# First layer's last MLP quarter by seven products, and the next layer's adaLN columns in the output projection, in a two-layer diffusion trunk

## The chip, the cores and the metric

One Trainium2 chip, one core. The time is device microseconds of one execution. TensorE (PE) multiplies, VectorE (DVE) and ScalarE (ACT) work on the operands and results, GpSimd (POOL) and SyncE (SP) issue transfers from HBM.

## What is computed

Two layers on 640 tokens (128 context and 512 latent) of width 1024, in fp32. Each layer is, cut to what matters here:

```
mod = silu(cond) @ w_ada[l] + b_ada[l]              # adaLN: sh1, sc1, g1, sh2, sc2, g2, 1024 each
h   = rms_norm(x, norm1_g) * (1 + sc1) + sh1
m   = mixers(h @ w_in)                               # FNet, GQA, differential attention, gated chunk MLP
x   = x + g1 * (sum(sigmoid(h @ w_gate) * branches) @ w_out)
h   = rms_norm(x, norm2_g) * (1 + sc2) + sh2
f   = square(relu(h @ w_mlp1)) @ w_mlp2              # 1024 -> 4096 -> 1024
x   = x + g2 * f
```

A final RMSNorm follows the second layer.

## The kernel before

**Tiles.** x is kept transposed in eight tiles `xT[m]` of 128 features by 640 tokens; HN = 320 is half the tokens. Every weight and operand is split into a rounded part and the rest, and each product of a block is three matmuls (`mm3`, line 807): high by high, low by high, high by low. So for every weight block of 128 x 1024 ACT makes a rounded copy (`whi`) and VectorE subtracts it to get `wlo`; `Stream.pump` (line 332) does this ahead. Weights come by SP into `raw` buffers. Those that a seven-product block needs as a sum of two blocks come into `chain` buffers, the second load adding to the first, issued on GpSimd's queue.

**The order of the work** is set by a planner at build time. Each engine has an estimated clock. The main program issues TensorE's matmuls. Generators in numbered lanes (norms, sums, attention, adaLN) are stepped from `tick` (line 617) whenever TensorE's clock has passed the time at which they are due; `tick` first lets the weight stream pump, then steps the lanes. What is issued later on an engine stands behind what was issued before.

**A layer.** First projection of h (`bq_bkv`, line 1010: query and key/value columns of branch B, token tile by token tile), other projections and attention, gates and branches, output projection (`units_of` for feature tiles 0 and 1, then `tail`, line 831, for tiles 2 to 7 in two halves of the tokens), norm, MLP.

**The MLP** has four quarters q of 1024 hidden columns. Each has a block m1 (by w_mlp1) and a block m2 (by w_mlp2). A block is a 2 x 2 matrix product by seven products p1 to p7 instead of eight (the Strassen-Winograd scheme; `block`, line 2064). A product is 48 matmuls of 320 columns: two pairs of output tiles, four inner tiles, three matmuls. Its operands p5, p6, p3, p7, p4 are sums of the operand's quarters, made and split by `sums` (line 1926) in a lane; p1 and p2 are quarters themselves (`hh`, `hl` of h; `fh`, `fl` of f). The order of the products is p1, p2, p5, p6, p7, p3, p4. `m1_read` squares the relu and makes the quarters of f; `m2_read` (line 2154) adds g2 times the result to xT.

**The exception** is m2 of q = 3. It is done plainly: the first four feature tiles by `units_of` (192 matmuls of 320 columns), the last four by `tail` with the token parts (0, 256) and (256, 640): 96 matmuls of 256 and 96 of 384 columns. m1 of q = 3 therefore makes `fhi` and `flo` for all of f instead of operands of seven products. In layer 0 the next layer's adaLN set 0 (its first 2048 columns: `ada_run`, line 701, eight steps of four matmuls, each with two loads of 512 KB issued two steps ahead, then four transposes and an addition) is spawned there and interleaves with the first 192 matmuls. The norm for the next layer (`norm_part`, line 764) starts for the first 256 tokens once their part is done. It is: sums of squares by TensorE (`ones,sq`), a reciprocal square root in twelve tiny VectorE operations on `small`, a broadcast by TensorE (`ident,small`), then for each of eight k `ht` (VectorE), `hhi` (ACT), `hlo` (VectorE). Layer 1's first projection takes token tiles 0, 1 and then 2, 3, 4.

**The norm before the MLP** (`mlp_rstd`, line 1978, and `mlp_h`) has the same steps for each half; the second half's are done during p1 of the first m1 block. All units of 128 x 1280 come from one pool of 30.

## Time and profile before

| | us |
|---|---|
| median of three runs (2069.89 to 2070.89) | 2069.9 |
| the profiled execution | 2070.2 |
| its span | 2068.4 |
| TensorE busy | 2009.4 (97%) |
| VectorE busy | 1322.5 (64%) |
| ACT busy | 1009.0 (49%) |
| GpSimd busy | 212.9 (10%) |

The span is the time between the first and the last instruction in the trace; the execution's own time is 1.8 us longer. A row of the table of stretches gives a stretch's limits, its length, each engine's busy time with the number of instructions, the granted TensorE clock (1.00 is the upper level, 2.4 GHz; a part of a stretch at 1.2 GHz lowers the mean), the DMA engines' busy share and what they moved. In layer 0 the output projection ends at 612.13 us, the first m1 block's p1, p2, p5, p6, p7 follow up to 659.12. The last m1 block's p4 begins at 961.84, plain m2 at 969.78, its `tail` at 1020.69, layer 1's first projection at 1049.85 and ends at 1082.04.

### The profile page before, as it was taken

Reading aid. Unit: us, or ns where it says so; the run is one execution under the profiler, and the core shown is the slowest. Engines: PE = TensorE matmul, PEld = TensorE weight load, DVE = VectorE, ACT = ScalarE, POOL = GpSimd, SP = SyncE. Lnnn points to the kernel's source line nnn. Section 1 sums busy time; section 2 is a strip of 40 time slices with the busy share of each in tenths; the row PEclk is TensorE's granted clock in tenths of the full one; section 3 lists DMA queues with packets and bytes.
Section 4 is the critical chain, followed back from the end, with each engine's and each line's share of the span. In section 5 each row is a group of like instructions: output and inputs, shape, how many; then the busy total and the mean of one; then the engine's idle time right before and its main releaser. Section 6 shows DMA issues by size and latency. Waiting matters only on the chain.

```text
span 2068.4 us, 35108 instructions
## 1 busy us (share of the span) xinstructions
PE 2009.4 (97%) x14404; PEld 1949.1 (94%) x14404; DVE 1322.5 (64%) x2370; ACT 1009.0 (49%) x1741; POOL 212.9 (10%) x245
## 2 busy tenths in 40 slices
PE   8999999999999999998999999999999999999998
PEld 7999999997898999998799999999979999999998
DVE  5765567863457858674466666777534577677654
ACT  4455444542347564745244544444323574747563
POOL 0000000001001221222100000000110012211200
PEclk9999999999999999999999999999999999999999
DMA  9421021347628899998321212123474378999841
GB/s 304 140 68 48 32 77 62 117 144 245 178 68 182 184 211 199 219 203 267 121 89 52 66 53 72 35 87 110 150 291 124 75 188 194 210 202 207 196 115 52
DMA packets 249762, 291.48 MB, mean 141 GB/s; under 512 B 11632, under 2 KB 214480, under 8 KB 249600
## 3 DMA queue, kind: packets, MB, share of 16 engines
q1 hardware_dynamic: 175952, 178.88, 26.6%
q0 software_dynamic: 73504, 110.29, 25.8%
q8 instruction: 113, 1.85, 0.4%
q14 instruction: 49, 0.40, 0.1%
q10 hardware_dynamic: 144, 0.07, 0.0%
HBM read 277.92 MB, written 11.27 MB: 140 GB/s over the span
## 4 chain that ended last, share of the span: by engine, by line
PE 90%; DVE 3%; DMA 2%; ACT 2%; SPq 2%; issue 1%; DVEq 0%; ACTq 0%
PE psum L131 90%; SPq L131 2%; DMA raw<-in_w_mlp_dram 1%; DMA p4s<-h_spill 1%; DMA raw<-in_w_gate_dram 1%; DVE wlo L131 1%; ACT whi L131 0%; DVE small L131 0%; DMA ada<-in_w_ada_dram 0%; DVE UV L131 0%; ACT UV L131 0%; DVE hq L131 0%; ACT L131 0%; DVE p5l L131 0%; DVE ht L131 0%
## 5 line engine op out<-in xcount | busy, mean ns | idle before, releaser
L131 DVE TENSOR_TENSOR wlo<-raw,whi 128x1024 fp32r<-128x1024 f32 (+1 forms) x270 | 311.7, 1158 | 131.3 <-ACT whi L131 129.6
L131 ACT CAST whi<-raw 128x1024 fp32r<-128x1024 f32 (+1 forms) x270 | 268.1, 995 | 153.2 <-PE psum L131 97.7
L131 PE MATMUL psum<-hhi,whi 128*128 128x320 f32 x1024 | 326.5, 319 | 0.1
L131 PE MATMUL psum<-hlo,whi 128*128 128x320 f32 x1024 | 317.0, 310 | 0.0
L131 PE MATMUL psum<-hhi,wlo 128*128 128x320 f32 x1024 | 316.8, 309 | 0.0
L131 PEld LDWEIGHTS psum<-hhi,whi 128*128 128x128 f32 x1024 | 193.0, 189 | 24.5 <-issue 21.8
L131 PE MATMUL psum<-whi,hhi 128*128 128x256 f32 x640 | 188.1, 294 | 6.3 <-DVE UV L131 4.5
L131 PEld LDWEIGHTS psum<-hhi,wlo 128*128 128x128 f32 x1024 | 193.3, 189 | 0.0
L131 PEld LDWEIGHTS psum<-hlo,whi 128*128 128x128 f32 x1024 | 192.8, 188 | 0.0
L131 PE MATMUL psum<-whi,hlo 128*128 128x256 f32 x640 | 181.6, 284 | 2.3 <-DVE hlo L131 2.0
L131 PE MATMUL psum<-wlo,hhi 128*128 128x256 f32 x640 | 180.8, 283 | 0.8 <-DVE wlo L131 0.8
L131 POOL DMA_DIRECT2D chain<-in_w_mlp_dram x84 | 108.0, 1290 | 435.0 <-DMA chain<-in_w_mlp_dram 225.9
L131 DVE TENSOR_TENSOR wlo<-chain,whi 128x1024 fp32r<-128x1024 f32 x84 | 102.2, 1223 | 73.8 <-ACT whi L131 73.3
L131 PEld LDWEIGHTS psum<-whi,hhi 128*128 128x128 f32 x640 | 122.0, 191 | 9.8 <-DVE UV L131 5.3
L131 ACT ACTIVATE gt<-psum 128x320 f32<-128x320 f32 x128 | 56.1, 438 | 151.7 <-PE psum L131 148.7
L131 PEld LDWEIGHTS psum<-whi,hlo 128*128 128x128 f32 x640 | 122.3, 191 | 4.6 <-DVE hlo L131 4.0
L131 PEld LDWEIGHTS psum<-wlo,hhi 128*128 128x128 f32 x640 | 122.1, 191 | 1.0 <-DVE wlo L131 1.0
L131 ACT CAST whi<-chain 128x1024 fp32r<-128x1024 f32 x84 | 87.7, 1049 | 44.1 <-DMA chain<-in_w_mlp_dram 44.1
L131 DVE TENSOR_REDUCE small<-psum 128x1 f32<-128x640 f32 (+1 forms) x108 | 82.4, 775 | 38.2 <-PE psum L131 36.4
L131 DVE SCALAR_TENSOR_TENSOR gt<-gt,psum 128x320 f32<-128x320 f32 x96 | 46.7, 486 | 88.5 <-PE psum L131 87.7
L131 ACT ACTIVATE sq<-xT 128x320 f32<-128x320 f32 (+2 forms) x64 | 30.0, 471 | 142.4 <-DVE xT L131 142.3
L131 ACT COPY ev<-psum 128x640 f32<-128x640 f32 x84 | 58.1, 692 | 70.9 <-PE psum L131 67.1
(372 smaller groups left out, 5633.2 us busy)
## 6 DMA issues: line engine op xcount, KB each, us to landing
chain<-in_w_mlp_dram POOLq DMA_DIRECT2D x84, 512.0 KB, 7.2
raw<-in_w_mlp_dram SPq DMA_DIRECT2D x41, 1024.0 KB, 7.7
ada<-in_w_ada_dram POOLq DMA_DIRECT2D x80, 512.0 KB, 6.1
raw<-in_w_gate_dram SPq DMA_DIRECT2D x24, 1024.0 KB, 5.2
raw<-in_w_mlp_dram SPq DMA_DIRECT2D x46, 512.0 KB, 5.8
chain<-in_w_mlp_dram SPq DMA_DIRECT2D x28, 512.0 KB, 4.3
raw<-in_w_mlp_dram POOLq DMA_DIRECT2D x28, 512.0 KB, 7.6
raw<-in_w_in_dram SPq DMA_DIRECT2D x24, 512.0 KB, 4.6
```

The costliest lines, as they stand in the source:

```text
L131: ins = f(*args, **kw)
```

## The change

Layer 0's last m2 quarter goes by seven products as well, in an order of its own (LAST): p1, p5, p6, p7, p3, p4, p2. The results for tokens 320 to 639 are complete after p3 (that is p1, p5, p6, p7, p3) and p4, those for tokens 0 to 319 only with p2. Squares are taken by pairs of feature tiles (`sq_pair`). The next norm's parts become (384, 640) and (0, 384), and layer 1's first projection takes tiles 3, 4 and then 0, 1, 2; the banks of tiles 3 and 4 are evacuated between the two. Layer 1's last quarter stays plain.

The next layer's adaLN set 0 is spawned in the gates behind the two other sets, so that its steps run at the gates' end and in the output projection. In `sums` p7 is made before p3, in every block of both layers. Between the output projection's tail and p7 of the first m1 block, and from the last m2 block to the first part of layer 1's first projection, the weight stream pumps after the lanes instead of before them (`urgent`). `results` works in place, with one buffer for each of p1, p5, p6 in the last block. At the start the token parts of the first norm change in the same way.

```diff
     ORDER = ("p1", "p2", "p5", "p6", "p7", "p3", "p4")
 
-    def square_chunks(tag, src, r0, c0):
+
+    LAST = ("p1", "p5", "p6", "p7", "p3", "p4", "p2")
...
-                square_chunks(("m2", l, q), w_mlp2[l], q * 1024, 0)
+            if q < 3 or l + 1 < L:
+                square_chunks(("m2", l, q), w_mlp2[l], q * 1024, 0, LAST if q == 3 else ORDER)
...
+    urgent = [False]
+
     def tick(pump=True):
-        if pump:
+        if pump and not urgent[0]:
             W.pump()
         going = True
         while going:
...
+        if pump and urgent[0]:
+            W.pump()
...
-    PARTS = ((0, 256), (256, T))
+    PARTS = ((384, T), (0, 384))
...
-    HPARTS = (((0, 0, 128), (1, 128, 256)), ((1, 256, T),))
+    HPARTS = (((1, 384, T),), ((0, 0, 128), (1, 128, 384)))
...
-
+    def norm_part(nl, which, part, done, first, come):
+
+        while not come(part):
+            yield when(lambda: 0.0 if come(part) else NEVER)
...
-            for tiles in ((0, 1), (2, 3, 4)):
+            for i, tiles in enumerate(((3, 4), (0, 1, 2))):
                 for k in range(KT):
-                    need(hts[tiles[0] // 2], k)
+                    need(hts[i], k)
                     bq_bkv(ss, k, tiles)
-                    if tiles[0] and k % 4 == 3:
+                    if i and k % 4 == 3:
                         for s in ss[k // 4 * 2:k // 4 * 2 + 2]:
                             W.done(s)
                     tick()
-                if tiles[0] == 0:
-                    out_of(XQ.f[:, 0:2, :], two(bank(2)))
-                    out_of(XK.f[:, 0:2, :], two(bank(3)))
+                urgent[0] = urgent[0] and i == 0
+                if i == 0:
+                    out_of(XQ.f[:, 3, :], bank(4, 256, 256))
+                    out_of(XK.f[:, 3, :], bank(5, 256, 256))
+                    out_of(XQ.f[:, 4, :], bank(0, 256))
+                    out_of(XK.f[:, 4, :], bank(0, 256, 256))
+        out_of(XQ.f[:, 0:2, :], two(bank(2)))
...
                     tA = spawn(5, ada_run(l, (1,), 7))
-                    spawn(5, ada_run(l, (2,), 7))
+                    tS = spawn(5, ada_run(l, (2,), 7))
+                    if l + 1 < L:
+                        spawn(5, ada_run(l + 1, (0,), 7))
...
-        finish_lane(5)
+        finish(tS)
         mul_a(l, 1)
...
             yield room(F)
             yield from split_unit(X, "p6", q11, after)
+            yield from by_rows(q12, lambda r: tt(q12.f[:, r], q22.f[:, r], q12.f[:, r], ALU.subtract))
+            yield room(F)
+            yield from split_unit(X, "p7", q12, after)
+            q12.drop()
             yield room(F)
             yield from split_unit(X, "p3", q22, after)
-            yield from by_rows(q12, lambda r: tt(q12.f[:, r], q22.f[:, r], q12.f[:, r], ALU.subtract))
             q22.drop()
             while (1, 0) not in F:
                 yield when(lambda: 0.0 if (1, 0) in F else NEVER)
@@ -1950,9 +1965,6 @@
             yield from by_rows(q21, lambda r: stt(q21.f[:, r], q11.f[:, r], -1.0, q21.f[:, r], ALU.mult, ALU.subtract))
             q11.drop()
             yield room(F)
-            yield from split_unit(X, "p7", q12, after)
-            q12.drop()
-            yield room(F)
             yield from split_unit(X, "p4", q21, after)
             q21.drop()
...
         def mlp_norm(part):
+            if part:
+                finish_lane(5)
             spawn(1, mlp_rstd(part))
             spawn(3 * part + 2, mlp_h(part))
...
         normed = []
-        tail(("out", l), g1, mh, ml, mlp_norm, HALVES)
+        urgent[0] = True
+        tail(("out", l), g1, mh, ml, mlp_norm)
...
 
-        def block(tag, X, read, before=None, over=None):
-
-            for P in ORDER:
-                grp = P in ("p2", "p5", "p3")
+        def block(tag, X, read, before=None, over=None, order=ORDER):
+
+            for P in order:
...
-        def m2_read(P, pp, a, b):
+        def m2_read(P, pp, a, b, last=False):
             def put(key, p, e, sign):
                 if e is not None:
-                    v = ev[2].f[:, rows2(pp)]
-                    tt(v, e, p, ALU.add)
-                    p = v
+                    tt(e, e, p, ALU.add)
+                    p = e
                 for j in range(2):
                     m = 4 * key[0] + 2 * pp + j
                     for cnd, c0, c1 in (((0, 0, 128), (1, 128, HN)), ((1, HN, T),))[key[1]]:
                         gt = g2[:, m, cnd:cnd + 1] if sign > 0 else ng.f[:, m - 4, cnd:cnd + 1]
                         xs, o = xT[m].f[:, c0:c1], HN * key[1]
                         stt(xs, p[:, j, c0 - o:c1 - o], gt, xs, ALU.mult, ALU.add)
-            results(P, pp, a, b, put)
+                if last:
+                    spawn(2, sq_pair(4 * key[0] + 2 * pp, key[1]))
+            if last:
+                results(P, pp, a, a if P == "p2" else b, put, (0, 1, 2))
+            else:
+                results(P, pp, a, b, put)
...
+            rows = q == 3 and l + 1 == L
...
+                if q == 0 and P == "p7":
+                    urgent[0] = False
+                if rows and P in ("p2", "p7"):
                     fhK.extend(kbufs("fhi", r=True, n=4))
...
-            if q < 3:
+            if not rows:
                 spawn(3, all_sums(FX, FQ))
-            block(("m1", l, q), HX, m1_read(FQ, FX, fhK if q == 3 else None, flK), before, over)
+            block(("m1", l, q), HX, m1_read(FQ, FX, fhK if rows else None, flK), before, over)
             if q < 3:
                 block(("m2", l, q), FX, m2_read, None, lambda P: drop_x(FX, P))
-        for i in (0, 1):
...
         if l + 1 < L:
+            sqacc, *sqt = sqb = kbufs("sq", n=4)
             ht = kbufs("ht", n=2)
-            spawn(5, ada_run(l + 1, (0,), 7))
+            hts = []
+            summed = [0, 0]
+            next_norm = norm_of(l + 1, 0, lambda part: summed[1 - part] == 4)
+            urgent[0] = True
+
+            def sq_pair(m, half):
+
+                c = hs_of(half)
+                first = not summed[half]
+                x, o, t = (two(b.buf.flat_f)[:, :, c] for b in (xT[m], sqb[0], sqb[2]))
+                yield soon("act", x)
+                afn(o if first else t, x, AF.Square)
+                if not first:
+                    yield soon("dve", t)
+                    tt(o, o, t, ALU.add)
+                if summed[half] == 3:
+                    yield soon("dve", o)
+                    tt(sqacc.f[:, c], sqacc.f[:, c], sqb[1].f[:, c], ALU.add)
+                summed[half] += 1
+
+            mul_a(l + 1, 0)
+
+            def before_last(P):
+                nonlocal hK, lK
+                if P == "p3":
+                    hK, lK = kbufs("hhi", r=True), kbufs("hlo", r=True)
+
+            def over_last(P):
+                drop_x(FX, P)
+                if P in ("p3", "p2"):
+                    hts.append(next_norm(len(hts)))
+
+            block(("m2", l, 3), FX, lambda *x: m2_read(*x, last=True), before_last, over_last, LAST)
+            drop_ev()
+            finish_lane(2)
         else:
+            drop_ev()
+            sqacc, *sqt = sqb = kbufs("sq", n=4)
             xg = kbufs("xg")
-        units_of(("m2", l, 3), range(4), fhK, flK, ev_res(g2, True) if l + 1 < L else ev_fin, 2, (1, 0))
-        if l + 1 < L:
-            hK, lK = kbufs("hhi", r=True), kbufs("hlo", r=True)
-            finish_lane(5)
-            mul_a(l + 1, 0)
-            hts = tail(("m2", l, 3), g2, fhK, flK, norm_of(l + 1, 0))
-        else:
+            units_of(("m2", l, 3), range(4), fhK, flK, ev_fin, 2, (1, 0))
             final_tail()
```

On TensorE, around the norm of the MLP: the end of p1 of layer 0's first m1 block (hh, hl by whi_87, wlo_91) and the start of p2 (whi_84), before:

```order
L131 MATMUL psum<-hh,wlo_91 128x320
L131 MATMUL psum<-hl,whi_87 128x320
L131 MATMUL psum<-ones,sq 64x1 x5
L131 MATMUL psum<-ident,small 128x64 x5
L131 MATMUL psum<-hh,whi_84 128x320
```

and now, the middle of p1 and its end:

```order
L131 MATMUL psum<-hh,wlo_90 128x320
L131 MATMUL psum<-hl,whi_86 128x320
L131 MATMUL psum<-ones,sq 64x1 x5
L131 MATMUL psum<-hh,whi_86 128x320
...
L131 MATMUL psum<-hh,wlo_91 128x320
L131 MATMUL psum<-hl,whi_87 128x320
L131 MATMUL psum<-ident,small 128x64 x5
L131 MATMUL psum<-hh,whi_84 128x320
```

The sums of squares moved from the end of p1 to behind its first 18 matmuls; 30 matmuls stand between them and the broadcast.

On TensorE, the end of layer 0, where part 0 of the next norm is broadcast, before (fhi, flo by the plain tail's weights; 66 more matmuls of 384 columns stand between this broadcast and the first one of layer 1's projection):

```order
L131 MATMUL psum<-fhi,wlo_89 128x384
L131 MATMUL psum<-flo,whi_85 128x384
L131 MATMUL psum<-ident,small 128x128 x2
L131 MATMUL psum<-fhi,whi_85 128x384
L131 MATMUL psum<-fhi,wlo_89 128x384
```

and now (fh, fl by p2's weights, then hhi, hlo by the projection's):

```order
L131 MATMUL psum<-fh,wlo_89 128x320
L131 MATMUL psum<-fl,whi_85 128x320
L131 MATMUL psum<-ident,small 128x128 x2
L131 MATMUL psum<-whi_86,hhi 128x256
L131 MATMUL psum<-whi_86,hlo 128x256
```

The broadcast moved to the boundary: the next matmul is the first that needs its result.

On VectorE at the same place, the twelve operations of part 0's reciprocal root and what follows, before:

```order
L131 TENSOR_SCALAR small<-psum 128x2
L131 TENSOR_SCALAR small<-small 128x2 x4
L131 TENSOR_TENSOR small<-small 128x2 x2
L131 SCALAR_TENSOR_TENSOR small<-small 128x2 x2
L131 TENSOR_TENSOR small<-small 128x2 x2
L131 SCALAR_TENSOR_TENSOR small<-small 128x2
L131 SCALAR_TENSOR_TENSOR xT<-psum,mods_72,xT 128x384
```

and now, from the root's eighth operation on (ev holds p1's result, to which p2 is added):

```order
L131 SCALAR_TENSOR_TENSOR small<-small 128x2 x2
L131 TENSOR_TENSOR small<-small 128x2
L131 TENSOR_TENSOR ev_6093<-ev_6093,psum 128x640
L131 SCALAR_TENSOR_TENSOR xT<-ev_6093,mods_72,xT 128x128
L131 SCALAR_TENSOR_TENSOR xT<-ev_6093,mods_72,xT 128x192
L131 SCALAR_TENSOR_TENSOR xT<-ev_6093,mods_72,xT 128x128
L131 SCALAR_TENSOR_TENSOR xT<-ev_6093,mods_72,xT 128x192
L131 TENSOR_TENSOR small<-small 128x2
L131 SCALAR_TENSOR_TENSOR small<-small 128x2
L131 TENSOR_TENSOR sq<-sq 128x2x320
L131 SCALAR_TENSOR_TENSOR ht<-xT,mulA_76,psum 128x256 x2
```

The root's last two operations now stand behind p2's last addition and updates of xT, which wait for p2's last matmul.

## Rows read from the trace of the kernel before

**Rows 1.** The page, busy time by engine (share of the span, instructions):

```profile
PE 2009.4 (97%) x14404; PEld 1949.1 (94%) x14404; DVE 1322.5 (64%) x2370; ACT 1009.0 (49%) x1741; POOL 212.9 (10%) x245
```

**Rows 2.** Table of stretches, layer 0, p1 to p7 of the first m1 block:

```profile
612.13:619.26 7.13, 7.13 (x50) 6.94 (x48) 5.27 (x8) 5.34 (x9) 0.58 (x1) 1.00 0.92 194
619.26:623.38 4.12, 2.00 (x21) 1.84 (x20) 2.87 (x13) 0.69 (x1) 0.70 (x1) 1.00 1.05 264
623.38:632.05 8.67, 8.67 (x49) 8.67 (x49) 6.46 (x8) 7.83 (x13) 2.55 (x2) 0.80 0.93 131
632.05:641.31 9.26, 7.57 (x51) 7.05 (x49) 9.06 (x11) 8.43 (x12) 2.39 (x2) 1.00 0.09 13
...
648.53:659.12 10.59, 8.83 (x50) 8.57 (x49) 7.64 (x9) 5.43 (x7) 1.32 (x2) 0.84 1.00 296
898.48:905.52 7.04, 7.04 (x50) 7.04 (x49) 5.76 (x8) 2.79 (x3) 1.28 (x1) 1.00 0.80 243
```

**Rows 3.** Table of stretches, layer 1, the sum of the same six:

```profile
sum 48.45, PE 42.90 PEld 41.53 DVE 37.62 ACT 33.39 POOL 10.30; mean PE 7.15 PEld 6.92 DVE 6.27 ACT 5.57 POOL 1.72
```

**Rows 4.** Table of stretches, layer 0's end and layer 1's first projection:

```profile
961.84:969.78 7.94, 7.30 (x50) 7.04 (x49) 7.67 (x9) 7.75 (x11) 3.13 (x6) 1.00 0.56 186
969.78:994.77 24.99, 17.10 (x92) 15.06 (x90) 9.41 (x12) 11.20 (x16) 2.10 (x4) 0.86 0.84 293
994.77:1020.69 25.92, 24.42 (x171) 16.72 (x171) 8.82 (x17) 5.64 (x10) 7.13 (x13) 1.00 0.34 100
1020.69:1049.85 29.16, 29.16 (x204) 29.16 (x202) 18.34 (x52) 9.86 (x21) 1.62 (x3) 1.00 0.33 116
1049.85:1082.04 32.19, 30.63 (x253) 30.23 (x253) 20.34 (x51) 11.91 (x20) 0.54 (x1) 1.00 0.22 67
1068.00:1080.00 12.00, 12.00 (x102) 12.00 (x101) 5.38 (x8) 3.66 (x5) 0.00 (x0) 1.00 0.22 61
1082.04:1084.29 2.25, 0.60 (x6) 0.36 (x4) 2.13 (x4) 2.22 (x6) 0.00 (x0) 1.00 0.00 0
```

**Rows 5.** Waits of TensorE, 605 to 660 us (in total, times, longest):

```profile
PE psum L131 <- DVE p7l L131: 1.8, 1, 1.8
PE psum L131 <- DVE p5l L131: 1.7, 2, 1.4
```

**Rows 6.** Waits of TensorE, 960 to 1090 us:

```profile
PE psum L131 <- ACT fhi L131: 5.2, 2, 4.6
...
PE psum L131 <- ACT XK L131: 1.7, 1, 1.7
```

**Rows 7.** Table of stretches: an adaLN step in the gates; the output projection's start:

```profile
476.30:477.31 1.01, 1.01 (x10) 0.16 (x9) 0.79 (x2) 0.00 (x0) 0.00 (x0) 1.00 0.00 0
567.58:588.70 21.12, 21.12 (x146) 21.12 (x145) 8.48 (x20) 3.77 (x7) 0.00 (x0) 1.00 0.16 50
```

**Rows 8.** The page, DMA issues (count, KB each, us to landing):

```profile
chain<-in_w_mlp_dram POOLq DMA_DIRECT2D x84, 512.0 KB, 7.2
...
ada<-in_w_ada_dram POOLq DMA_DIRECT2D x80, 512.0 KB, 6.1
```

**Rows 9.** Timeline of VectorE (start, length), the root before the MLP:

```profile
620.04 0.16 DVE L131 TENSOR_SCALAR small<-psum 64x5 f32<-64x5 f32 x1 [2.10 <-PE psum L131]
...
621.92 0.15 DVE L131 SCALAR_TENSOR_TENSOR small<-small 64x5 f32<-64x5 f32 x1
```

**Rows 10.** Groups of VectorE by shape, 960 to 1062 us (busy, mean ns | idle before):

```profile
L131 DVE TENSOR_TENSOR wlo<-raw,whi 128x1024 fp32r<-128x1024 f32 x14 | 17.1, 1223 | 11.4 <-ACT whi L131 11.1
...
L131 DVE SCALAR_TENSOR_TENSOR ht<-xT,mulA,psum 128x128 f32<-128x128 f32 x16 | 4.7, 342 | 0.0
...
L131 DVE TENSOR_TENSOR ev<-ev,psum 128x640 f32<-128x640 f32 x4 | 3.3, 815 | 0.0
...
L131 DVE SCALAR_TENSOR_TENSOR ht<-xT,mulA,psum 128x384 f32<-128x384 f32 x2 | 1.1, 613 | 0.0
```

**Rows 11.** Waits of TensorE, layer 1's gates, 1470 to 1485 us:

```profile
PE psum L131 <- DVE OC L131: 3.2, 1, 3.2
```

More of the change, by code (lines that the diff above doesn't have):

```diff
@@ L762, in h_low @@
             stt(lK[k].r[:, a:b], ht[k % 2].f[:, a:b], mods[nl].f[:, 24 * which + k, cnd:cnd + 1], hK[k].f[:, a:b], ALU.add, ALU.subtract)
-    def norm_part(nl, which, part, done, first):
+    def norm_part(nl, which, part, done, first, come):
+        while not come(part):
+            yield when(lambda: 0.0 if come(part) else NEVER)
         c0, c1 = PARTS[part]
@@ L788, in norm_part, with norm_of @@
         done.append(KT - 1)
-    def norm_of(nl, which):
+    def norm_of(nl, which, come):
         first = []
@@ L795, in f @@
             done = []
-            t = spawn(7 - part, norm_part(nl, which, part, done, first if part else ()))
+            t = spawn(7 - part, norm_part(nl, which, part, done, first if part else (), come))
             first.append(t)
@@ L827, in x_update, with tail @@
                 stt(xs, o[:, a - c0:b - c0], gch[:, m, cnd:cnd + 1], xs, ALU.mult, ALU.add)
-    HALVES = ((0, HN), (HN, T))
-    def tail(tag, gch, xhi, xlo, then, parts=PARTS):
-        m0 = 4 if parts is PARTS else 2
+    def tail(tag, gch, xhi, xlo, then):
         ss = {}
-        tasks = []
-        for part, (c0, c1) in enumerate(parts):
-            for m in range(m0, 8):
+        for half in range(2):
+            for m in range(2, 8):
                 if m not in ss:
                     ss[m] = W.get(tag + (m,))
-                o = bank(((0, 1, 2, 3), (4, 5, 0, 1))[part][m - 4] if m0 == 4 else m - 2, c1 - c0)
-                fm_part(ss[m], o, slice(c0, c1), xhi, xlo)
-                if part:
+                o = bank(m - 2, HN)
+                fm_half(ss[m], o, half, xhi, xlo)
+                if half:
                     W.done(ss[m])
-                x_update(m, gch, o, c0, c1)
-                sq_add(m, c0, c1)
-            tasks.append(then(part))
-        return tasks
+                x_update(m, gch, o, half * HN, half * HN + HN)
+                sq_add(m, half * HN, half * HN + HN)
+            then(half)
     ctx.enter_context(tc.manual_schedule())
@@ L1978, in mlp_rstd @@
         def mlp_rstd(part):
-            c0, c1 = HALVES[part]
+            c0, c1 = part * HN, part * HN + HN
             o = 400 + 8 * part
@@ L2062, in tile_hybrid_trunk @@
         dve.tensor_scalar(out=ng.f, in0=g2[:, 4:8, :], scalar1=-1.0, scalar2=None, op0=ALU.mult)
-        def block(tag, X, read, before=None, over=None):
-            for P in ORDER:
-                grp = P in ("p2", "p5", "p3")
+        def block(tag, X, read, before=None, over=None, order=ORDER):
+            for P in order:
+                grp = P in ("p2", "p5", "p3") and (order is ORDER or P != "p2")
                 if before is not None:
@@ L2302 @@
+            kdrop(flK)
 _INS = [
```

52 lines of the change are left out of this document (26 added, 26 removed).

## The prediction

> **What bounds the kernel now.** I began with the busy times over the span: TensorE is busy 2009.4 us, 97% of 2068.4 [rows 1]. So only two things can shorten the run: fewer or shorter matmuls, or taking away what interrupts them. Next I read the stretches the change touches, stage by stage, in the table of stretches: the out-projection's end with the first two MLP products of each layer [rows 2, 3], and the end of layer 0 [rows 4]. The undisturbed product in the last line of [rows 2] is the yardstick: 48 matmuls of 320 columns in 7.04 us, 0.147 us each, granted clock 1.00. A stage of one product that lasts longer has lost time in one of two ways. Either TensorE's busy time is below the stage's length (a wait, named in [rows 5, 6]), or the granted clock is below 1.00, part of the stage at the lower of the two levels (1.2 GHz instead of 2.4).
>
> **Term 1, adaLN columns, +9.9 us where they go.** Eight steps and four transposes leave the end of layer 0 (that gain lies in term 3). A step costs 1.01 us in the gates [rows 7]. 102 plain matmuls stand in the 25.92 us of the third line of [rows 4], 102 x 0.147 = 14.96; less 1.9 of waiting, 9.1 remain for steps and transposes. They cost the same in their new place. Their loads go into GpSimd's queue, which issues 512 KB apiece that land 6.1 us later [rows 8]. Two of the eight steps stand back to back there, 22 matmuls (3.2 us) after the step behind which the second's loads are issued. Waiting could cost 6.1 - 3.2 = 2.9; I take 0.8, since the DMA share in that stretch is only 0.16 and the 16 steps in the gates wait for nothing [rows 7]; ends 0 and 2.9. The Trainium skill ("DMA: Bandwidth & Descriptors", section "Anatomy of one DMA — SWDGE (gpsimd) path") fits such a transfer as 2.0 us plus bytes over 436 GB/s, 3.2 us for 512 KB. By that the double step would wait for nothing, and the term would be 9.1; the row's 6.1 is nearly twice that.
>
> **Term 2, out-projection to MLP, -10 us for both layers.** From the projection's end to p3, layer 0 takes 46.99 us (from 612.13 to 659.12, [rows 2], where p6's line from 641.31 to 648.53 is left out), where five products and about 1.9 for sums and broadcasts would take 37.1. The loss of 9.9 is: 2.1 idle for the reciprocal root of the norm (a chain of twelve small VectorE operations, 2.03 us by its first and last [rows 9]) and some 0.2 around it; 1.6 of low clock behind it (p2: 8.67); 2.2 for p5, mostly waits for p5l [rows 5], and 0.2 at p6; p7's 2.0, mostly for p7l [rows 5], and 1.5 at low clock. Layer 1 repeats it with 48.45 in sum [rows 3]. The change places the sums after 18 matmuls of p1 and 30 more (4.4 us) between them and the broadcast, so the chain and its issue fit under p1. It makes p7 before p3, so p7l comes one split (two copies, two subtractions) earlier. But p2 now starts some 2 us sooner, while p5l hangs on VectorE's norm updates and weight splits (wlo 1.22 us each [rows 10]), which are no shorter. Reckoned from p1's start, p2 ends at 15.4, p5l allows p5 at about 18.8, then come 0.7 of a second wait and 1.7 of low clock, and three products to 42.4. That is -4.6 here and, from 48.45, -6.0 in layer 1, of which 0.6 is kept back for small waits. Worst 0 (p5l later by all that is gained), best -14 (p5 waits as little as today).
>
> **Term 3, the last m2 quarter, -29.5 us.** The first four lines of [rows 4], from the last m1 product to the end of m2, add up to 88.01. Now: p4 of the last m1 block 7.04 (a wait of up to 0.9 stays, 0.7 taken), seven products 49.28, the first part's sums 0.36, and 1.1 where p6's weights are just split (one wlo): 58.5. Of the 29.5, 7.2 are fewer columns (a plain quarter is 192 matmuls of 0.147, 96 of 256 columns at 0.120 by the 102 in 12.00 us of [rows 4], and 96 of 384 at 0.175, which is what the fourth line leaves after 11.5 and 0.8 of sums and broadcasts: 56.5 against 49.28). 9.1 are the ada work, which term 1 gives back, and 1.9 its wait. 11.8 are the second line, 24.99 against 90 x 0.147 = 13.2: 7.9 idle, mostly for ACT's fhi [rows 6], and 3.9 of low clock (17.10 busy). Between two seven-product blocks fh and fl come out of the lane that has made every quarter so far; the undisturbed product at 898 [rows 2] is such a place. The Trainium skill ("TensorE: Matmul & The Clock Gate", section "Wait — 56ns, not 53.3ns?") puts a matmul at N/2.4 GHz plus about 2.5 ns, 135.8 ns for 320 columns. By it 48 fewer would be worth 6.5 instead of 7.0 us, but the rows show 146.7.
>
> **Term 4, the next layer's norm before its first projection, +7.0 us.** Until now 66 matmuls of 384 columns (11.6 us) stood between the first part's broadcast and the first projection matmul; the projection took 32.19 [rows 4], against 240 x 0.120 + 1.2 for sums and broadcast = 30.0 clean. Now the broadcast is the last thing before it, the root's last operations stand on VectorE behind the eight residual updates of p2, and behind the broadcast h must still be formed on VectorE, rounded on ACT and its rest taken on VectorE. Reckoned from p2's last matmul: the residual's adds and updates, with the root's last two, to 2.8 (one add of 0.82 [rows 10], then four updates), broadcast 3.4, h 3.9 (256 columns, between 0.34 for 128 and 0.61 for 384 [rows 10]), rounding and rest to 5.4. So about 5.5 us idle. An idle of 2.1 cost 1.6 of clock [rows 2] and 7.9 cost 3.9 [rows 4], so some 3 here; behind it three wlo (3.7 us) stand on VectorE ahead of the third row of h, overlapping that. Total 30.0 + 5.5 + 3.7 = 39.2. Best: 2 us idle, clock up, +2 less the old waits, about +3. Worst: the whole first pass (96 matmuls) at half clock behind the waits, +16.
>
> **Term 5, -1.7 us.** Behind the projection TensorE stood for ACT's XK [rows 6], in a stage of 2.25 us with 0.60 of work [rows 4]. Tiles 3 and 4 are now evacuated in the first pass, and the bank the next projection takes is free. Ends 0 and -1.7.
>
> **Term 6, -4 us.** In layer 1's gates TensorE waits 3.2 us for OC [rows 11]; the low clock behind an idle of 2.1 cost 1.6 [rows 2], so some 4 to 5 are lost there. In the changed order 72 gate matmuls stand ahead of OC's transpose instead of 30, as in layer 0, which has no such wait. Ends 0 and -5.
>
> **Term 7, +0.3 us.** At the start the last tiles are normed first, so rows of h that were 256 wide are 384 wide (0.61 us on VectorE [rows 10]); ends 0 and 0.8.
>
> **Sum.** 9.9 - 10 - 29.5 + 7.0 - 1.7 - 4 + 0.3 = -28.0, against the profiled execution's 2070.2 (2068.4 of span and 1.8 around it, which stay): 2042.2. That execution is 0.3 above the median of the runs, 2069.9, so the forecast for the median is 2041.9, or 2042.
>
> **Rivals.**
> *The norm's wait costs double.* The boundary is the one place where the change makes a wait. At the worst end of term 4 it is +16 instead of +7: 2051. For it: nothing lies between broadcast and projection. Against: idle near 5 us cost less clock than that elsewhere.
> *Term 2 yields nothing.* VectorE, not the norm, is what p5 waits for (9.06 of its 9.26 us busy [rows 2]). Then the idle and the low clock only move from p2 to p5, in both layers: 2052; with OC's wait too, 2056.
> *The waits between the blocks return.* If p1's, p5's or p6's operands and weights come as late as fhi did, the second line's 11.8 stand again in place of the 1.1: 2053. For it: weights for four of seven products come through accumulating loads of 7.2 us [rows 8], and p5 now stands one product sooner than in the other blocks.
> *The boundary is nearly hidden* (term 4 at +3, term 2 at -11): 2037.
> *The ada steps starve, slower than before.* If each of the eight waited for its own two loads in full, 8 x 6.1 = 48.8, 0.8 of it counted, the time is 2090. It decides from 3.6 us a step: (28.0 + 0.8) / 8 eats the whole gain, and 4.1 makes it slower by 0.2%. Against: the sixteen steps before them in the same queue run at 1.01 us [rows 7] without a wait.
> *The change does not do what it says*, its reordering being undone by the planner: excluded by the changed order of the instructions, which has 48 matmuls fewer and the ada steps in the projection.
>
> **How the numbers follow.** Chances: forecast (2039 to 2047) 0.47; the norm's wait 0.15; term 2 empty 0.13; waits between the blocks 0.09; boundary hidden, or several terms better (down to 2030) 0.12; something slower by the ada steps or a wait of that size 0.02; within the measurement's reach of no change 0.02. Leaving out the last two and the tails (above 2056, below 2032) gives 2032 to 2056. About 0.2%, 4.1 us, is what a measurement here can tell from no change: faster 0.96, same 0.02, slower 0.02.
>
> **What would show it.** Term 1: eight ada steps of 1.0 us in the projection before the MLP, with under 3 us of waiting. Term 2: no idle ahead of p2, an idle of 2 to 4 us ahead of p5, none ahead of p7. Term 3: seven products of 7.0 to 7.3 us where 80 us of plain matmuls and ada steps stood. Term 4: 4 to 7 us idle directly behind p2's last matmul, released by VectorE's small or hlo, then a stretch of granted clock below 1. Terms 5 and 6: no wait for XK, none for OC. It is wrong if the boundary shows more than 16 us over today, if p5's wait has taken all of the 2 us won at p2, or if a load, not an engine, ends the waits of the last block.

## The result, and the profile after

The changed kernel takes 2041.9 us (median, 2041.2 to 2044.4) against 2069.9: a ratio of 0.987, interval 0.985 to 0.988. That is 28.0 us less, the forecast to 0.1 us. The agreement is better than the reasoning behind it, and that it is so close is luck. One of the seven terms is off by 2.3 us and two more by 1.6 and 1.3, the misses cancel, and the largest term is right in size with the wrong cause, which the experiments show below.

The page of the changed kernel, busy time by engine: its span is 2040.5 us, 27.9 less, and TensorE is busy 14.1 us less ([rows 1]); the other 13.8 us were time in which TensorE did nothing.

```profile
PE 1995.3 (98%) x14356; PEld 1936.8 (95%) x14356; DVE 1338.8 (66%) x2389; ACT 1022.7 (50%) x1754; POOL 223.0 (11%) x253
```

The two traces, stage by stage (each stage runs from the first matmul of one group to the first of another; forecast and measured are changes in us):

| term, stage | forecast | measured |
|---|---|---|
| 1, first projection of layer 0 to the output projection's end | +9.9 | +9.3 |
| 2, from there to p3, layer 0 and layer 1 | -10 | -4.7 and -3.0 |
| 3, p4 of the last m1 block to m2's last matmul | -29.5 | -28.9 |
| 4, from there to the projection's end | +7.0 | +7.9 |
| 5, XK | -1.7 | -1.9 |
| 6, layer 1's projection to its output projection's end | -4 | -5.6 |
| 7, start | +0.3 | -1.0 |
| the rest of the two MLPs | 0 | +0.8 and -0.9 |

**Term 1.** In the table of stretches, the two adaLN steps of the gates' end that stand back to back (a single one takes 1.00 us):

```profile
557.99:559.84 1.85, 1.85 (x17) 0.41 (x17) 1.54 (x2) 1.85 (x3) 1.85 (x4) 1.00 0.92 121
```

The double step took 1.85 us without a wait, so the 0.8 kept for it was not needed. The adaLN loads of the whole run landed after 5.5 us (median of 80), not after the 3.2 us estimated from the fit in the Trainium skill ("DMA: Bandwidth & Descriptors", section "Anatomy of one DMA — SWDGE (gpsimd) path"). That nothing waited therefore does not bear the estimate out.

**Term 2.** The same stretches in layer 0 (p1, p2, p5, p7; p6 between them took 7.04), then in layer 1 those of p5 and p7 and the sum, to be held against [rows 2, 3]:

```profile
620.50:628.85 8.35, 8.26 (x60) 7.59 (x58) 7.25 (x20) 5.31 (x7) 1.72 (x2) 1.00 0.60 147
628.85:637.85 9.00, 8.57 (x59) 8.23 (x59) 7.18 (x9) 7.05 (x12) 2.17 (x2) 1.00 1.13 236
637.85:648.67 10.82, 8.70 (x49) 8.43 (x49) 9.50 (x13) 9.65 (x14) 2.55 (x2) 0.84 0.53 81
...
655.71:662.75 7.04, 7.04 (x51) 7.04 (x49) 6.45 (x8) 5.84 (x8) 0.00 (x0) 1.00 0.89 256
...
1628.09:1640.27 12.18, 10.06 (x48) 9.79 (x49) 10.25 (x14) 9.43 (x14) 1.40 (x2) 0.72 0.81 164
...
1647.31:1656.23 8.92, 7.30 (x51) 7.04 (x49) 7.33 (x8) 5.12 (x6) 0.00 (x0) 1.00 0.81 272
sum 45.49, PE 41.22 PEld 39.69 DVE 38.14 ACT 33.42 POOL 7.65; mean PE 8.24 PEld 7.94 DVE 7.63 ACT 6.68 POOL 1.53
```

The idle ahead of p2 is gone, p7 runs in 7.04, and p5 has a wait, 2.1 us idle and 1.7 at the lower clock (granted 0.84). 42.25 us in all stand against 42.4 forecast, but in other shares: p2 ends 17.4 us after p1's start instead of 15.4, and p5 then starts sooner behind it than was reckoned. Layer 1 was taken to be the same. It is not: in this execution its p5 stays longer at the lower clock (granted 0.72), and p7 waits 1.6 us for a wlo, a weight split. The waits of TensorE there:

```profile
PE psum L131 <- DVE p5l L131: 2.1, 1, 2.1
PE psum L131 <- DVE wlo L131: 1.6, 1, 1.6
```

A second trace of the same kernel (e10_after_again) has the same waits ahead of p5 and p7, but other clocks. Its p5 in layer 0 and in layer 1:

```profile
637.72:647.26 9.54, 7.41 (x48) 7.15 (x49) 8.68 (x12) 9.48 (x14) 2.12 (x2) 1.00 0.61 92
1626.78:1637.78 11.00, 8.88 (x49) 8.62 (x49) 10.14 (x14) 9.43 (x14) 1.38 (x2) 0.84 0.81 146
```

In layer 0 the same 2.1 us of idle are followed by a granted clock of 1.00 here and of 0.84 in the first trace. The five stretches of each layer add up to 40.96 and 44.31 us in it, 6.0 and 4.1 less than before. So what a wait costs at the lower clock differs from one execution to the next by more than a microsecond, and the wait for wlo is the part of the miss that both traces show.

**Terms 3 to 5.** The stretches of layer 0's end: p4 and p1, p5, p6, then p7, p3 and p4, then p2 to its last matmul, from there to the projection's first matmul, its first 48 matmuls with sums, the rest, and the four transposes behind it (to be held against [rows 4]):

```profile
966.30:980.38 14.08, 14.08 (x98) 14.08 (x97) 12.56 (x16) 12.85 (x19) 3.87 (x3) 1.00 1.15 262
980.38:988.53 8.15, 7.21 (x50) 6.94 (x48) 7.24 (x11) 6.35 (x10) 1.28 (x1) 1.00 0.89 136
988.53:996.79 8.26, 7.41 (x48) 7.19 (x49) 5.35 (x5) 4.12 (x5) 6.17 (x9) 1.00 0.67 99
996.79:1017.91 21.12, 21.12 (x146) 21.12 (x145) 18.45 (x27) 11.47 (x13) 1.47 (x3) 1.00 0.61 179
1017.91:1025.40 7.49, 7.49 (x54) 7.38 (x52) 5.84 (x21) 3.24 (x4) 1.08 (x2) 1.00 0.43 149
1025.40:1029.94 4.54, 0.86 (x6) 0.52 (x4) 4.23 (x12) 1.52 (x4) 2.46 (x5) 0.91 0.60 243
1029.94:1042.42 12.48, 11.05 (x60) 10.46 (x61) 11.73 (x31) 4.33 (x8) 0.74 (x2) 0.62 0.67 243
1042.42:1065.54 23.12, 23.12 (x195) 23.12 (x194) 14.02 (x37) 10.85 (x21) 0.00 (x0) 1.00 0.12 32
1065.54:1065.89 0.35, 0.35 (x6) 0.35 (x5) 0.27 (x1) 0.27 (x2) 0.00 (x0) 1.00 0.00 0
```

Nothing waits for the operands of this quarter any more, and XK's wait is gone. Two short waits are left, both for p6's first weights: 0.9 us for their rounding (at the end of p5's stretch) and 0.8 for their split. The new wait is where term 4 put it: 3.7 us idle between p2 and the projection, then more in the projection's first 48 matmuls, which have a mean granted clock of 0.62. The waits of TensorE from 960 to 1070 us name the chain, the root's `small`, then `hhi`. Of the two for wlo, the longer one is at the boundary and the other is p6's:

```profile
PE psum L131 <- DVE small L131: 2.5, 1, 2.5
PE psum L131 <- DVE wlo L131: 2.0, 2, 1.1
PE psum L131 <- ACT hhi L131: 1.2, 1, 1.2
```

### The profile page after: what moved, and what is told of

It reads as the page before. It is cut to its first block, busy times and chain, and to the rows that moved or that the text cites. A ratio compares the mean times of both kernels' runs of the same rounds, so it can differ in the third digit from the quotient of the medians.

```text
span 2040.5 us, 35045 instructions
## 1 busy us (share of the span) xinstructions
PE 1995.3 (98%) x14356; PEld 1936.8 (95%) x14356; DVE 1338.8 (66%) x2389; ACT 1022.7 (50%) x1754; POOL 223.0 (11%) x253
## 4 chain that ended last, share of the span: by engine, by line
PE 90%; DVE 5%; ACT 3%; DMA 1%; issue 1%; POOL 0%; ACTq 0%; SPq 0%; DVEq 0%; POOLq 0%
PE psum L131 90%; DVE wlo L131 1%; DMA chain<-in_w_mlp_dram 1%; ACT whi L131 1%; DMA raw<-in_w_mlp_dram 0%; DVE ht L131 0%; DVE xT L131 0%; DVE fq L131 0%; ACT fq L131 0%; DVE UV L131 0%; ACT UV L131 0%; DVE small L131 0%; ACT L131 0%; DMA xtok<-in_x_prompt_dram 0%; ACT hq L131 0%
## 5 line engine op out<-in xcount | busy, mean ns | idle before, releaser
L131 DVE TENSOR_TENSOR wlo<-chain,whi 128x1024 fp32r<-128x1024 f32 x90 | 109.9, 1224 | 92.5 <-ACT whi L131 91.6
L131 POOL DMA_DIRECT2D chain<-in_w_mlp_dram x90 | 116.2, 1291 | 412.7 <-DMA chain<-in_w_mlp_dram 226.8
L131 ACT CAST whi<-chain 128x1024 fp32r<-128x1024 f32 x90 | 94.2, 1049 | 30.5 <-DMA chain<-in_w_mlp_dram 30.4
L131 ACT COPY ev<-psum 128x640 f32<-128x640 f32 x90 | 62.2, 691 | 70.3 <-PE psum L131 69.9
L131 ACT CAST PThi<-psum 128x640 fp32r<-128x640 f32 x64 | 44.4, 694 | 93.2 <-PE psum L131 89.8
```

The costliest lines, as they stand in the source:

```text
L131: ins = f(*args, **kw)
```

## The experiments

### The adaLN columns alone

```diff
-                    spawn(5, ada_run(l, (2,), 7))
+                    tS = spawn(5, ada_run(l, (2,), 7))
+                    if l + 1 < L:
+                        spawn(5, ada_run(l + 1, (0,), 7))
...
-        finish_lane(5)
+        finish(tS)
...
-            spawn(5, ada_run(l + 1, (0,), 7))
```

> The kernel before with one part of the change alone: the next layer's adaLN set 0 runs behind the other two sets (gates' end and output projection) instead of in layer 0's last m2 quarter, which stays plain. Theory FORM (that of the prediction): the 11.8 us lost in the plain quarter's first 90 matmuls belong to its form, fhi and flo made late by ACT and VectorE. Then the waits for fhi stay (7 to 8 us idle, 3 to 4 of low clock), only the 1.9 us wait for the adaLN copy goes: 2068 us, ratio 0.999, 0.998 to 1.000. Rival LOAD: in the kernel before one weight load issued at 969.15 landed only at 981.28, beside nine adaLN loads of 512 KB issued from 964 to 971, and ACT's queue stood 7.5 us behind its whi. Then those waits go with the adaLN loads: 90 matmuls in 13.2 to 16 us instead of 24.99, 2056 to 2060 us, ratio 0.993 to 0.995.

Measured: 2056.4 us, ratio 0.995 (0.993 to 0.997), span 2052.8, which is 15.6 below the profile of before. By the runs it is 0.5%, 11 us (7 to 15), so part of the 15.6 is the choice of the two executions. The plain quarter's first 192 matmuls, and TensorE's waits from there to layer 1's first projection:

```profile
978.35:1007.11 28.76, 28.42 (x195) 28.16 (x193) 13.07 (x20) 11.06 (x16) 1.63 (x3) 1.00 0.43 142
```

```profile
PE psum L131 <- ACT XK L131: 1.7, 1, 1.7
...
PE psum L131 <- DVE flo L131: 0.3, 1, 0.3
```

The 192 plain matmuls take 28.76 us where 24.99 + 25.92 stood (9.1 of that adaLN work, 1.9 the wait for its copy), and fhi is not waited for, in the same plain form. FORM, the reason given in the prediction, falls. LOAD holds. What LOAD says is read in the trace of the kernel before: ACT's timeline has a rounding of weights that waits 7.53 us for its load, with fhi behind it.

```profile
973.07 0.68 ACT L131 ACTIVATE ev<-psum 128x640 f32<-128x640 f32 x1
981.29 1.04 ACT L131 CAST whi<-raw 128x1024 fp32r<-128x1024 f32 x1 [7.53 <-DMA raw<-in_w_mlp_dram]
982.24 0.73 ACT L131 ACTIVATE fhi<-ev 128x640 fp32r<-128x640 f32 x1
```

The DMA issues of the kernel before from 963 to 975 us, and of this one from 963 to 985 (KB each, median us to landing):

```profile
ada<-in_w_ada_dram POOLq DMA_DIRECT2D x9, 512.0 KB, 7.0
...
raw<-in_w_mlp_dram SPq DMA_DIRECT2D x2, 512.0 KB, 12.0
```

```profile
raw<-in_w_mlp_dram SPq DMA_DIRECT2D x2, 512.0 KB, 8.0
```

### The loads without the steps

```diff
+    def loads_only(l, sets):
...
+            yield pe_at([u.f for u in ada_in[l, s, k]])
+            for x in ada_in.pop((l, s, k)):
+                x.drop()
+            if i + 2 < len(steps):
+                ada_load(l, *steps[i + 2])
...
+            spawn(5, loads_only(l + 1, (0,)))
```

> The kernel of e1_ada_moved with the sixteen loads of the adaLN set issued once more in layer 0's last quarter, as in the kernel before, and nothing computed from them (no adaLN step, copy or transpose there). Theory LOAD: the loads alone hold up the weight loads next to them, so most of the 11.8 us comes back in the last quarter: 2064 to 2069 us. Rival STEPS: it was the steps, the copy or the lane's order that made fhi late; then the loads cost nothing, 2055 to 2058 us.

Measured: 2072.9 us, ratio 1.001 (1.000 to 1.002), span 2073.3. The 192 plain matmuls again, the DMA issues from 975 to 1000 us, and ACT's timeline:

```profile
983.03:1024.69 41.66, 32.55 (x194) 30.96 (x193) 14.88 (x22) 13.40 (x20) 7.07 (x13) 0.88 0.68 223
```

```profile
ada<-in_w_ada_dram POOLq DMA_DIRECT2D x10, 512.0 KB, 9.6
...
raw<-in_w_mlp_dram SPq DMA_DIRECT2D x2, 512.0 KB, 19.6
```

```profile
995.48 1.04 ACT L131 CAST whi<-raw 128x1024 fp32r<-128x1024 f32 x1 [10.04 <-DMA raw<-in_w_mlp_dram]
996.43 0.73 ACT L131 ACTIVATE fhi<-ev 128x640 fp32r<-128x640 f32 x1
```

Sixteen transfers of which nothing is computed cost 13 us by the ratios of the two kernels to the kernel before (0.995 and 1.001), 16 by the medians; STEPS falls. Two weight loads take 19.6 us (median) beside them instead of 8.0, ACT stands 10.04 us at the rounding of one, and fhi, whose relu was done before, stands behind it. That it costs more than LOAD expected (2064 to 2069) goes with a load that is later than in the kernel before (19.6 against 12.0 us): here no steps stand between the loads. Late weight loads beside the adaLN loads are the cause of the largest loss in the kernel before.

### p7 ahead of p3 alone

```diff
             yield from split_unit(X, "p6", q11, after)
+            yield from by_rows(q12, lambda r: tt(q12.f[:, r], q22.f[:, r], q12.f[:, r], ALU.subtract))
+            yield room(F)
+            yield from split_unit(X, "p7", q12, after)
+            q12.drop()
...
-            yield room(F)
-            yield from split_unit(X, "p7", q12, after)
-            q12.drop()
```

> The kernel before with one part of the change alone: in the sums p7 is made before p3, in all blocks. Theory ORDER (that of the prediction): the wait of 2.0 us for p7l and the 1.5 us of low clock behind it go in both layers, p2 and p5 stay as they are: 7 us less, 2063 us, ratio 0.9966. Rival QUEUE: VectorE has the same work and is late as a whole, so the wait moves to p3 or p4: 2 us less at most, ratio 0.999 to 1.000.

Measured: 2064.5 us, ratio 0.998 (0.997 to 0.999), so 4.6 us of the 7 are left by the runs, between the two expectations. The profiled execution is the slowest of the ten (2070.3 us, span 2068.5), and in it nothing is left. In both layers p7 of the first block went from 10.59 to 7.04, and p5 stayed (9.25): ORDER holds there. In layer 0 the gain of this execution was spent on a slower broadcast ahead of p2 (1.2 us), on waits and lower clock in the blocks behind (2.2), and in the last m1 block, whose p3, p4 and first 90 plain matmuls are these stretches:

```profile
954.17:967.57 13.40, 7.20 (x50) 6.94 (x48) 2.38 (x3) 2.71 (x5) 2.63 (x5) 0.92 1.00 397
967.57:983.38 15.81, 9.93 (x48) 9.53 (x49) 10.46 (x12) 12.74 (x17) 1.06 (x2) 0.63 0.64 201
983.38:996.68 13.30, 13.30 (x93) 13.11 (x91) 5.00 (x7) 4.99 (x7) 1.58 (x3) 1.00 0.67 217
```

They take 42.5 us together; before, 7.04 + 7.94 + 24.99 = 40.0. The waits that make up most of it left fhi and went to p4's operand (p4h 6.2, p4l 5.9 us), in a stretch in which the DMA engines are full (share 1.00, 397 GB/s). Neither expectation foresaw that, and how often it happens is not known from one trace. It fits LOAD, the adaLN set's transfers meeting whatever load is next in line, but was not taken apart in this kernel.

### The pump ahead of the lanes again

```diff
-            urgent[0] = True
+            urgent[0] = False
```

(at both places)

> The changed kernel with one part undone: the weight stream always pumps ahead of the lanes (urgent is never set). Theory URGENT: VectorE's splits of weights (1.22 us each) stand in the chains of the norm again, so an idle of 1 to 2 us and some 1.5 of low clock come back ahead of p2 in each layer, and the boundary to layer 1 grows by one to three splits: 4 to 8 us slower than the changed kernel, 2046 to 2050 us. Rival PLACE: that the sums stand 30 matmuls ahead of the broadcast hides the root whatever stands in between; then 0 to 1 us slower, 2042 to 2043 us.

Measured: 2045.0 us, ratio 0.989 (0.987 to 0.991), span 2042.6. The changed kernel has 0.987 and, a second time, 0.988, with intervals that overlap this one: 2 to 5 us slower, not clear of noise, between the two theories or at the lower end of URGENT. With the pump ahead, the planner puts the sums back to p1's end, and behind p2's: place and urgency are one thing, not rivals. Layer 0 takes 44.64 us from p1 to p3 (42.25 and 40.96 in the two traces of the changed kernel), layer 1 45.02 (45.49 and 44.31), the boundary 41.7 from p2's last matmul to the projection's end (40.1 and 41.0). So only layer 0 lies clear of both traces, by 2.4 us or more. Where the idle ahead of p2 returns (2.1 us for `small` in layer 0), p5's wait shrinks (1.4 and 0.3 instead of 2.1).

### One product ahead instead of two

```diff
-    LAST = ("p1", "p5", "p6", "p7", "p3", "p4", "p2")
+    LAST = ("p1", "p5", "p6", "p7", "p4", "p3", "p2")
```

> The changed kernel with the last block in the order p1, p5, p6, p7, p4, p3, p2: tokens 320 to 639 are complete one product (7.04 us) before the end instead of two. Theory AHEAD: the lead of two products is what lets the sums stand inside p2; with one, the sums and the root fall behind p2's last matmul, the boundary grows by 2 to 5 us, 2044 to 2047 us. Rival QUEUE: the broadcast waits for p2's residual updates on VectorE in any case, so the lead beyond one product is not used: 0 to 1 us, 2042 to 2043 us.

Measured: 2049.4 us, ratio 0.990 (0.989 to 0.992), span 2048.0. From p2's last matmul to the projection's first, then its first pass:

```profile
1026.80:1035.04 8.24, 1.82 (x9) 1.44 (x8) 7.31 (x23) 1.29 (x3) 3.20 (x6) 0.72 0.86 330
1035.04:1048.58 13.54, 10.05 (x49) 9.46 (x49) 8.09 (x26) 3.83 (x7) 0.00 (x0) 0.54 0.18 63
```

Boundary and projection take 46.3 us instead of 40.1: AHEAD, by somewhat more than expected. Of the 6.2 us, 3.7 are in the gap, 1.1 in the first pass (granted 0.54), and 1.4 behind it. QUEUE falls: the lead of half the tokens is worth 6 us.

### All but the seven products

```diff
+        urgent[0] = True
...
+                if q == 0 and P == "p7":
+                    urgent[0] = False
```

(beside the diffs of e1_ada_moved and e2_p7_first)

> The kernel before with the adaLN set moved, p7 made before p3 and the lanes ahead of the pump from the output projection to p7 (the parts b, c and d of the change), but with layer 0's last quarter plain as before. Theory NOTHING NET: seven products save 5.8 us up to p2's last matmul against the plain quarter without adaLN loads (e1_ada_moved: 64.9 us; changed kernel: 59.1), win 1.9 at XK, and lose 7.9 in the norm that is no longer covered, so this kernel is as fast as the changed one but for the wait for OC in layer 1's gates (up to 5.6 if it stays): 2042 to 2047 us. Rival EARNED (term 3 of the prediction as it was written): the seven products earn 7.2 in columns and 11.8 in waits, so without them 2055 us or more.

Measured: 2052.7 us, ratio 0.992 (0.991 to 0.994), span 2052.6: outside both expectations. OC's wait stayed, and the last m1 block's p4 took 12.70 us, with a wait of 3.4 us for p4l, which is made from p4h. ACT's timeline shows the two halves of p4h, 6.85 us apart:

```profile
965.24 0.71 ACT L131 CAST p4h<-p4s 128x640 fp32r<-128x640 f32 x1
965.85 1.05 ACT L131 CAST whi<-raw 128x1024 fp32r<-128x1024 f32 x1
...
970.68 0.74 ACT L131 ACTIVATE fhi<-ev 128x640 fp32r<-128x640 f32 x1
...
972.09 0.71 ACT L131 CAST p4h<-p4s 128x640 fp32r<-128x640 f32 x1
```

Between them the planner has put the plain quarter's relu and fhi and two roundings of weights. So the plain form can cost a wait, by the planner's order on ACT, but in another place than the one that it was blamed for.

### The plain quarter in the new order of tokens

```diff
-    PARTS = ((0, 256), (256, T))
+    PARTS = ((384, T), (0, 384))
...
+            for i, tiles in enumerate(((3, 4), (0, 1, 2))):
```

(beside the diff of e6_all_but_seven; with HPARTS and the early evacuation as in the change. `urgent` is not set at the boundary, where the norm is covered by the plain `tail`.)

> The kernel of e6_all_but_seven with the token order of the change as well: the next norm's parts (384, 640) and (0, 384), tiles 3 and 4 first in layer 1's projection and evacuated between its passes. Only the last quarter's seven products are missing from it. Theory NOTHING NET AT THE END: from the last m1 block's p4 to the end of layer 1's first projection's evacuation it takes what the changed kernel takes (99 to 100 us) if p4 runs undisturbed, or 5.7 more if ACT's second half of p4h again stands behind the plain quarter's fhi; the XK wait (1.9) is gone without any seven products; the wait for OC (4.2 and the low clock behind it) stays, since the planner puts 30 matmuls ahead of it as before. Time 2044 to 2052 us. Rival ORDER OF TOKENS: the wait for OC and the norm's waits hang on the token order; then OC's wait goes and the time is 2040 to 2044 us.

Measured: 2048.8 us, ratio 0.991 (0.989 to 0.992), span 2045.6. The stretches from p4 of the last m1 block: p4, plain m2, projection, transposes; then TensorE's waits in layer 1's gates:

```profile
967.68:976.93 9.25, 7.57 (x50) 7.04 (x49) 6.73 (x9) 7.86 (x11) 0.00 (x0) 1.00 0.79 251
976.93:1034.17 57.24, 57.24 (x394) 57.24 (x393) 30.85 (x66) 19.15 (x31) 3.80 (x7) 1.00 0.33 115
1034.17:1066.42 32.25, 30.82 (x253) 30.28 (x253) 21.33 (x61) 13.59 (x26) 0.54 (x1) 1.00 0.22 66
1066.42:1066.78 0.36, 0.36 (x7) 0.36 (x5) 0.24 (x1) 0.33 (x2) 0.00 (x0) 1.00 0.00 0
```

```profile
PE psum L131 <- DVE OC L131: 3.2, 1, 3.2
```

99.1 us, where the changed kernel takes 99.6 (966.30 to 1065.89). NOTHING NET holds: at the end of layer 0 the seven products take 5.2 us less than the plain quarter (52.1 against 57.2), p4 ahead of them takes 2.2 less, and 7.9 are given back in the uncovered norm and the lower clock. Had p4 run undisturbed in the plain kernel, the seven products would have lost 2.7 there. XK's wait goes with the early evacuation, without any seven products. What the seven products still bring is OC: the wait of 3.2 us stands in the traces of the kernels with the plain quarter (before, e1_ada_moved, e2_p7_first, e6_all_but_seven and this one) and not in those of the changed kernel, e3_pump_first, e4_p3_late and e5c_fill_again, and layer 1's stage is 4.1 us shorter (544.85 against 548.99). Why the planner's clocks stand so, and put more gate matmuls ahead of OC's transpose, was not traced.

### Work in the boundary

```diff
-                    tA = spawn(5, ada_run(l, (1,), 7))
+                    tA = spawn(5, ada_run(l, (1,) if l == 0 else (), 7))
...
+                if P == "p2":
+                    fill_step(3)
...
                     need(hts[i], k)
+                    if i == 0 and k == 0:
+                        fill["step"](3)
+                        fill["load"](2)
+                    if i == 1 and k in (0, 2):
+                        fill["step"](1)
```

> The changed kernel with work put into the boundary: the eight adaLN steps of layer 1's set 1 leave the end of layer 1's gates; three of them stand between p2's last matmul and the broadcast, three between the broadcast and the first projection matmul, two in the projection's second pass. Theory IDLE: the 2.5 + 1.5 + 1.1 us for which TensorE waits there and the low clock behind them are idle and nothing more, so six steps of 1.0 us cost almost nothing there: 5 to 7 us faster than the changed kernel, 2035 to 2037 us. Rival TRAFFIC: 6 MB of loads in the last two products make the projection's weights late, or the steps only push the broadcast and the norm behind them further back: 0 to 2 us faster, 2040 to 2042 us, or slower.

> As e5_fill, with the eight adaLN steps summed in a bank that the norm's second broadcast does not write. Theory IDLE: the time of e5_fill, 5 to 7 us below the changed kernel in the same session, 2034 to 2037 us. Rival TRAFFIC: 0 to 2 us, 2040 to 2042 us.

> The kernel of e5b_fill on the same chip and in the same session as the changed kernel: 5 to 7 us below it if the boundary's waits are idle and nothing more, 0 to 2 us if not.

> The changed kernel once more, beside the others on the same chip: 2040 to 2044 us, and the same waits in its trace (p5l 2.1 in each layer, small 2.5 and hhi 1.2 at the boundary).

In e5_fill the bank of the sums is overwritten by the norm's second broadcast, so layer 1's set 1 is not the model's; the kernel took 2036.7 us. With a bank of their own for the steps it took 2036.2 (e5b_fill), and once more 2034.0 (2031.6 to 2035.8; ratio to the kernel before 0.984, 0.982 to 0.986), beside 2041.6 for the changed kernel (e10_after_again; 0.988, 0.986 to 0.990, with the waits expected of it). The diff above is that of e5b_fill and e5c_fill_again. The stretches of e5c_fill_again from p2's last matmul to the projection's first, its first 48 matmuls, and the rest:

```profile
1027.08:1034.88 7.80, 6.14 (x54) 1.88 (x53) 6.76 (x18) 3.10 (x7) 4.03 (x8) 1.00 1.04 417
1034.88:1044.80 9.92, 7.86 (x65) 7.24 (x61) 9.46 (x26) 4.37 (x7) 0.83 (x2) 1.00 0.94 347
1044.80:1070.71 25.91, 25.91 (x215) 23.97 (x214) 14.95 (x40) 11.75 (x23) 0.00 (x0) 1.00 0.11 33
```

43.6 us with all eight steps and their transposes in it, where the changed kernel takes 40.1 or, in its second trace, 41.0 without them; layer 1's stage behind it is 9.8 us shorter (535.0 against 544.8). The granted clock stays at 1.00 throughout. The first two stretches, with six of the steps, take 17.7 us, and 17.0 or 17.9 in the changed kernel, so the six steps cost less than 1 us of time there. IDLE holds, by somewhat more than expected (7.6 us). This kernel is the fastest of the study.

## Why the prediction was right, and where it was not

**Term 1 was right**, its reserve for loads unneeded; the rival of starving steps is excluded by the row above.

**Term 2 was mis-sized by 2.3 us** in the first trace; in the second it measured -10.2 against -10, so the size of the miss is within what two executions differ by. The sum held in layer 0 within 0.2 us, with p2 2 us later and p5's wait that much shorter than reckoned. "p2 ends at 15.4" was too early by its own terms: two products of 7.04 and the 1.9 for sums and broadcasts make 16.0, and 0.5 of idle and 0.8 more for sums and broadcast came on top. The step that failed is "from 48.45, -6.0 in layer 1": layer 1 was taken as a copy of layer 0, but its p7 weights are split 1.6 us late in both traces, and its p5 runs at the lower clock for longer. The 1.6 of low clock that the sum takes for an idle of 2.1 is one outcome of several: the same idle ahead of p5 cost between 0.4 and 3.0 in the four stretches shown. The rival in which term 2 yields nothing is refuted in this kernel, but e3_pump_first shows what it was made of: part of the idle that is won ahead of p2 returns ahead of p5.

**Term 3 had the right size and the wrong cause.** The sum, 58.5, was measured as 59.1: p6's weights were waited for 1.8 us instead of 1.1, and the 0.7 kept for p4 was not needed. The step that failed is the one on the 11.8 us: "Between two seven-product blocks fh and fl come out of the lane that has made every quarter so far". The form was not the cause. The adaLN loads were (e1_ada_moved takes them away and the plain form does not wait, e7_loads_only puts them back alone and it waits more). So the accounts of the parts must be redrawn. By the ratios of the runs, moving the adaLN set alone is worth 0.5%, 11 us (15.6 by the spans of the traces), not the 1.9 of its copy less 0.8. The sums, the lanes and the order of tokens bring 0.4% more, 8 us (7.2 by the spans; e9_plain_order). The seven products bring the last 0.3%, 6 us beside e10_after_again (5.1 by the spans of the first traces, 4.1 of it in layer 1's stage with OC and nothing where they stand). The forecast of this term came out because both parts were in the change, which is luck. Had they been offered apart, it would have been wrong on each.

The row that could have told was in reach: the DMA share of 0.84 and 293 GB/s in the second line of [rows 4], and behind fhi's wait an ACT that itself waited for a load. I stopped at the engine that TensorE waited for, and did not ask what that engine waited for.

**Term 4 was right** (7.9 for 7.0, 8.8 in the second trace), idle and low clock in the place and order described, though the idle directly behind p2 is 3.7 us where 5.5 were reckoned, with 1.4 more in the first 48 matmuls; e4_p3_late shows that the lead of two products is what keeps it this small, e5c_fill_again that it is idle and nothing else.

**Terms 5 and 6** came as forecast, term 6 with 5.6 instead of 4: e9_plain_order, which still waits for OC, has 1.5 of it too (548.99 against 550.46). **Term 7** had the wrong sign: the start is 1.0 us shorter, all of it within the first 19 us of the span; it was not followed up.

**Among the rivals**, "the waits between the blocks return" did not occur: p5's and p6's stretches in the last block took 1.1 and 1.2 us longer than a clean product, and engines, not loads, ended the waits. But its fear, weights that come late, was the right one for the kernel before.

## What to carry to other kernels

When an engine waits for another, follow the second engine's wait too before you call its work the cause: in an in-order queue, an operand that was ready stands behind a weight rounding whose transfer is late. A bulk transfer belongs where no load that is needed next shares the DMA engines with it, even if the work on it costs the same everywhere. And a part that takes matmuls away just ahead of a norm gives them back if those matmuls were the norm's cover; put work there that has to be done anyway. When a sum takes a price of the lower clock from one execution, give it a range: look at a second trace of the same kernel.

## What the runs showed of the hardware

Loads of 512 KB on GpSimd's queue, of which nothing was computed, slowed two 512 KB loads on SP's queue from 8.0 to 19.6 us (medians of e1_ada_moved and e7_loads_only); ten of them stood in the same 25 us, with some 400 GB/s moved in all. The two queues in that stretch (packets, MB, share of the time of the 16 engines):

```profile
q0 software_dynamic: 1750, 5.96, 71.4%
q1 hardware_dynamic: 2515, 1.79, 22.0%
```

The Trainium skill ("DMA: Bandwidth & Descriptors", section "Queues, rings and completion order") says that each DMA engine takes turns between the queues that have work, a packet at a time. The trace agrees that the queues share the engines, but not evenly in time: GpSimd's queue took 71.4% and SP's 22.0%. GpSimd's packets are also larger, 3.4 KB on average against 0.7 KB, so turns by the packet could give such shares; no run here separates the two.

The granted clock stayed at 1.00 through 1.7 us of idle between adaLN steps (e5c_fill_again), and had a mean of 0.62 in the 12.5 us behind 3.7 us of idle (the changed kernel). The length of an idle alone did not decide it: 2.1 us ahead of p5l were followed by 0.84 in one trace of the changed kernel and by 1.00 in another, and the 3.2 us for OC by 0.58 in the kernel before (over 4.0 us) and by 1.00 in e9_plain_order (over 5.4 us):

```profile
1480.08:1484.10 4.02, 4.02 (x18) 4.02 (x19) 0.83 (x1) 1.42 (x2) 0.53 (x1) 0.58 0.34 99
1462.59:1468.00 5.41, 5.41 (x38) 5.41 (x39) 2.27 (x3) 3.15 (x5) 0.53 (x1) 1.00 0.30 97
```
